# Query, value, embedding and output products issued between attention blocks, and xT moved by 1,088 bytes

## The chip, the cores and the metric

The kernel runs on one core of one Trainium2 chip. The metric is the time of one execution on the device in microseconds (us), as a median of several runs. Engines: TensorE (PE in the profile, PEld for its weight loads), VectorE (DVE), ScalarE (ACT), GpSimd (POOL), SyncE (SP, which here issues the DMAs).

## The reference

A decoder trunk of two layers on 1,024 tokens of width 1,024, in float32. Layer 0 mixes tokens with a causal convolution module, layer 1 with sliding-window attention (window 128, blocks of 128 tokens, 16 query heads on 4 key-value heads of width 64, a learned sink per head). After each mixer come a layer norm, a squared-ReLU MLP, a layer norm and a gated embedding. The attention:

```python
def swa_sink_attention(x, w_q, sinks, w_o, kk, vv, cos, sin):
    q = partial_rope((x @ w_q).reshape(B, T, N_HEADS, HEAD_DIM), cos, sin)
    q = q.reshape(B, nb, BLOCK, N_KV_HEADS, Q_PER_KV, HEAD_DIM)
    scores = jnp.einsum("bnqkgd,bnskd->bnkgqs", q, kk) * (1.0 / math.sqrt(HEAD_DIM))
    scores = jnp.where(mask, scores, -jnp.inf)
    lse = jnp.logaddexp(jax.nn.logsumexp(scores, axis=-1, keepdims=True), sink)
    probs = jnp.exp(scores - lse)
    out = jnp.einsum("bnkgqs,bnskd->bnqkgd", probs, vv)   # vv: previous and own block
    return out.reshape(B, T, N_HEADS * HEAD_DIM) @ w_o
...
x = layer_norm(DEEPNORM_ALPHA * x + y, mix_ln_g[i], mix_ln_b[i])
x = layer_norm(DEEPNORM_ALPHA * x + sq_relu_mlp(x, mlp_w_up[i], mlp_w_down[i]), ...)
x = x + (p[i] @ ple_w_proj[i]) * jax.nn.sigmoid(x @ ple_w_gate[i])
```

## The kernel before, in words

Precision. Each float32 operand is split into a high and a low part (`split`, `prep`: a rounded copy on ACT, the difference on VectorE), and a product is three matmuls per tile of 128 rows (`mm3`: high by high, high by low, low by high). `xTh` and `xTl` hold the transposed activations, 8 x 1,024 columns each; `wh` and `wl` are five slots each for prepared weights, taken in order from one stream (`ws.add`, `ws.get`, `ws.done`).

Order. The kernel's text is not the order of issue. Every operation, including the allocation of each buffer, is recorded, and a planner in the kernel (`schedule`) goes through them with costs per operation, picking for each free engine the ready operation that stands earliest in the text. The result is a fixed order for each engine's queue, which the chip then follows in order. So where an operation stands in the text sets its priority: what stands later is used where nothing earlier is ready. All instructions are issued from one helper line, 454 in the profile of before, so groups are told apart by buffers.

Attention before. Key and query weights are laid out so that a weight unit gives 128 rows: two units for the rotated parts, three (`rest(0)`) for heads 0 to 7, three (`rest(1)`) for heads 8 to 15. `part_rows(u, h)` makes one product of 24 matmuls for one half h of the tokens (512); `keep_query` scales and splits it and stores it to DRAM (`qdh`, `qdl`, buffers A). Values (`vf`, buffers g) are eight products of 24 matmuls with 256 columns, one per 128 tokens. Then three PSUM banks pass from the tag `ps` to the blocks (`sc`, `pv`).

The blocks run in two passes, gp = 0 for heads 0 to 7 and gp = 1 for heads 8 to 15, each over eight blocks n of 128 tokens and two groups of four heads. For one block and group: `load_queries` (X, from DRAM, high part in the lower 64 partitions and low part in the upper), `load_keys` (E), `load_values` (v and bo), `scores` (matmuls ps<-E,X; a copy, a predicated copy, two reduces, four exponentials, a reciprocal, four scalings into z), and, one step later, `values` (four transposes ident,z; split to A; a masked copy by GpSimd; four matmuls A by v and bo; adds into t). Pass 0 stores its result to DRAM (`adh`, `adl`), since xT is still needed by the query products; pass 1 writes to rows 4 to 7 of xT directly.

Between the passes stands `rest(1)`. After both, the result of pass 0 is loaded into rows 0 to 3 of xT, the embedding product of layer 1 is made (`embed`, 16 tiles of six matmuls, stored to `proj`), the residual x is loaded (`xsp` to B and A), and `mix_out` makes the output product: first columns 0 to 511 (cc 0) for all pairs of token tiles, then columns 512 to 1,023 (cc 1), each followed by the residual add, the second by the layer norm.

Constants (`cst`, `ident`, `mhalf`) lie just below xTh and xTl in SBUF.

## Time and profile before

| | us |
|---|---|
| median of 3 runs | 2252.42 (2250.50 to 2253.15) |
| the profiled execution, its own time | 2252.04 |
| its span, first to last instruction | 2250.3 |
| TensorE busy | 2190.7 (97%) |
| VectorE busy | 1651.6 (73%) |
| ACT busy | 891.4 (40%) |
| GpSimd busy | 244.7 (11%) |

Busy shares are averages over stages. The span in slices shows each engine's share in tenths in 40 equal stretches of 56 us; PEclk is the clock that TensorE was granted. A wait is put down to what ended it. Matmuls are pipelined and their ends are modelled, so busy TensorE time may hold less work than it seems.

### The profile page before, as it was taken

What the parts mean: (1) busy time and instruction counts of PE and PEld (TensorE: products, weight loads), DVE (VectorE), ACT (ScalarE), POOL (GpSimd) and SP (SyncE); (2) the same over time, 40 slices, a digit from 0 to 9 for tenths busy, and PEclk for the clock granted to TensorE, in tenths of its full rate; (3) what the DMA queues carried; (4) which work ended last, traced back from release to release, by engine and by line L of the source; (5) the groups of instructions that cost most, each with busy time, mean ns of one, the idle gap of its engine ahead of it and who ended that gap; (6) DMA issues with size and microseconds to landing.
All of it is one profiled execution on the core that took longest, in us unless ns stands there. A gap on an engine that the chain in (4) does not pass through costs nothing.

```text
span 2250.3 us, 28661 instructions
## 1 busy us (share of the span) xinstructions
PE 2190.7 (97%) x10187; PEld 1804.0 (80%) x10187; DVE 1651.6 (73%) x2478; ACT 891.4 (40%) x1552; POOL 244.7 (11%) x431
## 2 busy tenths in 40 slices
PE   9999999999999999999999777999999999999999
PEld 7888878888888888888889555788888888888887
DVE  7666777977778887898454839379677779778983
ACT  5233433444443333444324727334344433333341
POOL 0000134100000000003001616032000000000040
PEclk9999999999999999999999879999999999999999
DMA  7444632244449644523565472423344486454322
GB/s 224 115 109 99 193 111 90 89 164 148 152 157 329 215 141 160 187 75 103 170 195 152 132 217 80 146 86 125 115 152 150 154 285 242 166 169 164 116 68 99
DMA packets 188704, 339.95 MB, mean 151 GB/s; under 512 B 19216, under 2 KB 84240, under 8 KB 188560
## 3 DMA queue, kind: packets, MB, share of 16 engines
q1 hardware_dynamic: 187264, 337.32, 46.4%
q8 instruction: 80, 1.31, 0.2%
q10 hardware_dynamic: 1296, 0.79, 0.1%
q14 instruction: 64, 0.52, 0.1%
HBM read 234.23 MB, written 103.81 MB: 150 GB/s over the span
## 4 chain that ended last, share of the span: by engine, by line
PE 45%; DVE 5%; DMA 2%; ACT 1%; issue 1%; SPq 0%; POOL 0%; ACTq 0%; DVEq 0%
PE ps L454 29%; PE tr L454 15%; DVE sm L454 1%; DVE A L454 1%; DVE t L454 1%; DVE xTl L454 1%; ACT z L454 1%; DVE z L454 0%; DVE B L454 0%; DVE wl L454 0%; DMA qdh<-A 0%; DMA X<-qdl 0%; DMA proj<-t 0%; ACT t L454 0%; DMA X<-qdh 0%
## 5 line engine op out<-in xcount | busy, mean ns | idle before, releaser
L454 PE MATMUL ps<-xTl,wh 128*128 128x512 f32 x744 | 295.7, 398 | 0.0
L454 PE MATMUL ps<-xTh,wl 128*128 128x512 f32 x744 | 295.0, 397 | 0.0
L454 PE MATMUL ps<-xTh,wh 128*128 128x512 f32 x744 | 294.3, 397 | 0.1
L454 DVE TENSOR_TENSOR wl<-raw,wh 128x1024 fp32r<-128x1024 f32 (+2 forms) x138 | 152.7, 1107 | 127.6 <-ACT wh L454 126.8
L454 PE MATMUL ps<-xTl,xTh 128*128 128x512 f32 x618 | 240.4, 389 | 0.0
L454 PE MATMUL ps<-xTh,xTl 128*128 128x512 f32 x618 | 240.4, 389 | 0.0
L454 PE MATMUL ps<-xTh 128*128 128x512 f32 x618 | 240.4, 389 | 0.0
L454 ACT CAST wh<-raw 128x1024 fp32r<-128x1024 f32 (+2 forms) x138 | 128.9, 935 | 278.4 <-PE ps L454 124.7
L454 PEld LDWEIGHTS ps<-xTh,wh 128*128 128x128 f32 x744 | 140.4, 189 | 32.9 <-ACT xTh L454 0.9
L454 PEld LDWEIGHTS ps<-xTh,wl 128*128 128x128 f32 x744 | 140.2, 188 | 32.4
L454 PEld LDWEIGHTS ps<-xTl,wh 128*128 128x128 f32 x744 | 140.1, 188 | 31.7 <-DVE xTl L454 0.2
L454 POOL TENSOR_SCALAR sm<-sm 128x1 f32<-128x1 f32 x40 | 14.5, 363 | 1387.1 <-DVE sm L454 1385.5
L454 PE MATMUL ps<-wl,xTh 128*128 128x512 f32 (+1 forms) x392 | 150.5, 384 | 0.0
L454 PE MATMUL ps<-wh,xTh 128*128 128x512 f32 (+1 forms) x392 | 150.0, 383 | 0.3 <-ACT xTh L454 0.3
L454 PE MATMUL ps<-wh,xTl 128*128 128x512 f32 (+1 forms) x392 | 149.8, 383 | 0.0
L454 PEld LDWEIGHTS ps<-xTh,xTl 128*128 128x128 f32 x618 | 116.1, 188 | 24.1
L454 PEld LDWEIGHTS ps<-xTh 128*128 128x128 f32 x618 | 116.0, 188 | 24.1
L454 PEld LDWEIGHTS ps<-xTl,xTh 128*128 128x128 f32 x618 | 116.0, 188 | 24.0
L454 ACT CAST xTh<-wh 128x1024 fp32r<-128x1024 f32 x74 | 77.4, 1046 | 123.1 <-PE ps L454 56.8
L454 DVE TENSOR_TENSOR wl<-g,wh 128x512 fp32r<-128x512 f32 x100 | 66.5, 687 | 74.0 <-ACT wh L454 74.0
L454 ACT CAST wh<-g 128x512 fp32r<-128x512 f32 x100 | 59.8, 620 | 152.3 <-PE ps L454 67.3
L454 DVE TENSOR_TENSOR E<-cst,g 128x1152 fp32r<-128x1152 f32 x64 | 86.1, 1353 | 45.1 <-PE ps L454 44.2
(285 smaller groups left out, 4973.4 us busy)
## 6 DMA issues: line engine op xcount, KB each, us to landing
wh<-hid SPq DMA_DIRECT2D x76, 512.0 KB, 4.2
raw<-in_w_up_dram SPq DMA_DIRECT2D x64, 512.0 KB, 3.5
wl<-in_w_down_dram SPq DMA_DIRECT2D x64, 512.0 KB, 4.6
hid<-zz SPq DMA_DIRECT2D x84, 256.0 KB, 2.8
hid<-t SPq DMA_DIRECT2D x78, 256.0 KB, 2.1
raw<-hid SPq DMA_DIRECT2D x34, 512.0 KB, 3.8
B<-scr SPq DMA_DIRECT2D x32, 256.0 KB, 4.1
t<-proj SPq DMA_DIRECT2D x32, 256.0 KB, 3.4
```

What stands on the lines that cost most here:

```text
L454: getattr(getattr(nc, o.eng), o.name)(*a, **k)
```

## The change

In the text of `attention`, work moves from before, between and after the blocks to places inside the loop over blocks:

- The query products of heads 0 to 7 are made for the first token half ahead of the blocks, and for the second half (`rest(0, n, (1,))`) after blocks 0, 1 and 2 of pass 0. Since each weight unit is now used twice, three units are loaded and prepared a second time.
- Two of the eight value products come ahead of the blocks, the other six after blocks 0, 2 and 4.
- The query products of heads 8 to 15 come after blocks 3, 4 and 5 of pass 0, the embedding product (its copies now in buffers B) and the residual loads of tiles 0 to 3 after block 7.
- The result of pass 0 is loaded into xT block by block inside pass 1.
- In pass 1 the first half of the output product (cc 0) starts: tiles 0 and 1 after block 2, tiles 2 and 3 after block 4. The remaining pairs and cc 1 follow the blocks.
- `cst` grows from 272 to 544 columns, of which the added ones are not used. Thereby xTh moves from byte 162,624 of each partition to 163,712, and xTl from 195,392 to 196,480.

```diff
+CST = 256 + NT * 32 + 2 * NH
...
-        self.cc = self.const("cst", (P, 256 + NH), F32)[:, 0 : 32 + 64 + CG]
+        self.cc = self.const("cst", (P, CST), F32)[:, 0 : 32 + 64 + CG]
...
-        ws.add(*[d["w_k"][k] for k in range(2)], *[d["w_q"][k] for k in range(5)], *[d["w_v"][k] for k in range(2)])
-        ws.add(*[d["w_q"][k] for k in range(5, 8)])
+        unit = d["w_q"]
+        ws.add(*[d["w_k"][k] for k in range(2)], *[unit[k] for k in range(5)], *[d["w_v"][k] for k in range(2)])
+        ws.add(*[unit[k] for k in range(2, 8)])
...
-        def rest(s):
-            for c in range(1, 4):
-                u = ws.get(1)[0]
-                for h in range(2):
-                    self.keep_query(self.part_rows(u, h), 1 + 3 * s + c, s * HT + c, 4, h)
-                ws.done(1)
+        def rest(s, c, halves):
+            u = ws.get(1)[0]
+            for h in halves:
+                self.keep_query(self.part_rows(u, h), 2 + 3 * s + c, s * HT + c + 1, 4, h)
+            ws.done(1)
...
+        def beside(gp, n):
+            if gp == 0:
+                if n < 3:
+                    rest(0, n, (1,))
+                if n % 2 == 0 and n < 6:
+                    value_rows(n + 2)
+                    value_rows(n + 3)
+                    if n == 4:
+                        ws.done(2)
+                if 3 <= n < 6:
+                    rest(1, n - 3, (0, 1))
+                if n == 7:
+                    self.embed(1, (0, 1), "B")
+                    self.load_residual(range(0, 4))
+                return
+            if n == 1:
+                ws.add(*[d["w_o"][0, u] for u in range(4)])
+                self.ou = ws.get(4)
+            if n in (2, 4):
+                self.out_tiles(0, PAIRS[n // 2 - 1], self.ou)
...
             for n in range(NT):
                 tk = slice(n * P, (n + 1) * P)
+                if gp:
+                    for x, v in zip((self.xTh, self.xTl), self.ad):
+                        nc.sync.dma_start(
+                            x.bitcast(F32)[:, 0:4, tk], v.rearrange("p (k t) -> p k t", k=4)[:, :, tk]
+                        )
                 keys = self.load_keys(n, gp)
...
-            if gp == 0:
-                rest(1)
+                beside(gp, n)
         self.values(*pend)
...
-        self.embed(1, (0, 1), "t")
...
-        self.mix_out(1, d["w_o"], gb, range(NT))
+        self.load_residual(range(4, 8))
+        for g in PAIRS[2:]:
+            self.out_tiles(0, g, self.ou, last=g is PAIRS[-1])
+        ws.add(*[d["w_o"][1, u] for u in range(4)])
+        us = ws.get(4)
+        for g in PAIRS:
+            self.out_tiles(1, g, us, gb, last=g is PAIRS[-1])
+
+    def out_tiles(self, cc, g, us, gb=None, last=False):
+        nc = self.nc
+        for ps, t in zip(self.tok_group(g, us, last=last), g):
+            xt = self.x[t][cc]
+            nc.vector.scalar_tensor_tensor(out=xt, in0=xt, scalar=ALPHA, in1=ps, op0=ALU.mult, op1=ALU.add)
+            if cc:
+                self.layer_norm(t, gb, self.mid[1])
```

More of the change, by code (lines that the diff above doesn't have):

```diff
@@ L1408, in attention @@
         nc, d, ws = self.nc, self.d, self.ws
-        ac = self.sb("cst", n=256 + NH)
+        ac = self.sb("cst", n=CST)
         nc.sync.dma_start(ac[:, 0:256], d["aconst"])
@@ L1426, in attention, with value_rows @@
         ws.done(4)
-        def rest(s):
-            for c in range(1, 4):
-                u = ws.get(1)[0]
-                for h in range(2):
-                    self.keep_query(self.part_rows(u, h), 1 + 3 * s + c, s * HT + c, 4, h)
-                ws.done(1)
-        rest(0)
+        def rest(s, c, halves):
[3 more added lines that the diff above has]
+            ws.done(1)
+        for c in range(3):
+            rest(0, c, (0,))
         vf = [self.sb("g") for j in range(4)]
-        us = ws.get(2)
-        for t in range(NT):
+        vu = ws.get(2)
+        def value_rows(t):
             ps = self.ps()[:, 0:256]
             self.mm3(ps, [
-                (*self.xs(kb, t * P, P), *[w[:, kb % 4 * 256 : (kb % 4 + 1) * 256] for w in us[kb // 4]])
+                (*self.xs(kb, t * P, P), *[w[:, kb % 4 * 256 : (kb % 4 + 1) * 256] for w in vu[kb // 4]])
                 for kb in range(KB)
@@ L1444, in attention @@
             nc.scalar.copy(vf[t // 2][:, t % 2 * 256 : (t % 2 + 1) * 256], ps)
-        ws.done(2)
+        for t in range(2):
+            value_rows(t)
         moves = ("ps", "sc"), ("ps", "sc"), ("ps", "pv"), ("bo", "v"), ("bo", "v")
@@ L1449, in attention @@
             nc.move(a, b)
+        def beside(gp, n):
[18 more added lines that the diff above has]
+                self.out_tiles(0, PAIRS[n // 2 - 1], self.ou)
+        self.x = [None] * NT
         pend = None
@@ L1468, in attention, with load_residual @@
             nc.move(b, a)
-        for q in range(4):
-            tk = slice(q * 256, (q + 1) * 256)
-            for x, v in zip((self.xTh, self.xTl), self.ad):
-                nc.sync.dma_start(x.bitcast(F32)[:, 0:4, tk], v.rearrange("p (k t) -> p k t", k=4)[:, :, tk])
-        self.embed(1, (0, 1), "t")
-        self.x = []
-        for t in range(NT):
-            xt = [self.sb("BA"[t // 4]) for q in range(2)]
-            for q in range(2):
-                nc.sync.dma_start(xt[q], self.xsp[t // 4][t % 4 * P : (t % 4 + 1) * P, q * HT : (q + 1) * HT])
-            self.x.append(xt)
         self.hid_tags = ("X", "E")
         gb = self.load_row("g", d["mix_g"][1:2]), self.load_row("g", d["mix_b"][1:2])
-        self.mix_out(1, d["w_o"], gb, range(NT))
+        self.load_residual(range(4, 8))
[5 more added lines that the diff above has]
+            self.out_tiles(1, g, us, gb, last=g is PAIRS[-1])
+    def load_residual(self, tiles):
+        nc = self.nc
+        for t in tiles:
+            self.x[t] = [self.sb("BA"[t // 4]) for q in range(2)]
+            for q in range(2):
+                nc.sync.dma_start(self.x[t][q], self.xsp[t // 4][t % 4 * P : (t % 4 + 1) * P, q * HT : (q + 1) * HT])
+    def out_tiles(self, cc, g, us, gb=None, last=False):
+        nc = self.nc
+        for ps, t in zip(self.tok_group(g, us, last=last), g):
[3 more added lines that the diff above has]
+                self.layer_norm(t, gb, self.mid[1])
     def scores(self, n, g, q, keys):
```

## The prediction

> **What bounds the kernel now.** I read the page first: busy times, then the span in slices.

> ```profile
> span 2250.3 us, 28661 instructions
> PE 2190.7 (97%) x10187; PEld 1804.0 (80%) x10187; DVE 1651.6 (73%) x2478; ACT 891.4 (40%) x1552; POOL 244.7 (11%) x431
> PE   9999999999999999999999777999999999999999
> DVE  7666777977778887898454839379677779778983
> PEclk9999999999999999999999879999999999999999
> ```

> TensorE bounds the kernel everywhere but in slices 23 to 25, about 1,240 to 1,400 us: the attention blocks. There alone its share falls to 7 tenths and the granted clock falls with it. VectorE reads 8, 3, 9 there: first and last slice full of blocks, the middle one without. So I cut the trace into stretches (busy time of each engine in each stretch). A product takes 24 matmuls; a "unit" below is one block of 128 tokens with one group of four heads, 32 units in two passes of 16.

> ```profile
> 1178.30:1483.40 305.10, 256.46 (x1249) 207.54 (x1248) 173.91 (x364) 148.28 (x392) 91.62 (x221) 0.90 0.50 144
> 1217.75:1275.77 58.02, 47.51 (x243) 37.63 (x242) 51.04 (x114) 43.50 (x124) 32.05 (x79) 0.92 0.59 155
> 1324.00:1339.71 15.71, 1.32 (x7) 0.76 (x5) 3.49 (x9) 2.11 (x7) 0.00 (x0) 0.61 1.10 275
> 1339.71:1391.45 51.74, 39.58 (x191) 30.75 (x192) 45.83 (x105) 38.31 (x115) 29.85 (x75) 0.85 0.48 120
> 1428.50:1483.40 54.90, 54.90 (x241) 45.06 (x240) 19.02 (x23) 7.93 (x9) 0.00 (x0) 1.00 0.26 83
> ```

> Columns: length, then busy us and count of PE, weight loads, DVE, ACT, POOL, then clock, DMA share, GB/s. The first row is the stretch that the change rewrites. Its start, 1178.30, is where the two built programs part: the same number of query and key products lies before it in both. Its end, 1483.40, is a point with the same work behind it in both: the first half of the output product (cc 0, eight tiles) and the first pair of the second half are done. Rows two and four are the first and the second pass of blocks: VectorE busy 88% and 89%, TensorE 82% and 76% at a reduced clock. So in the blocks VectorE sets the pace. Row three is a plain stall: the wait table names it.

> ```profile
> PE ps L454 <- DMA X<-qdl: 14.4, 1, 14.4
> ```

> The second pass waits 14.4 us for its queries, which go through DRAM.

> **The change, part by part.** It moves TensorE work that needs nothing from the blocks into the blocks: three query products of the second token half, six of the eight value products, six query products of heads 8 to 15, the embedding product (96 matmuls), and half of the output product. No product is dropped or added. So the sum is the length of the same stretch, made from TensorE's and VectorE's work. Prices at full clock come from the chain of waits, which lists runs of matmuls back to back:

> ```profile
> 1195.30 2.83 PE tr L454 x24
> 1310.10 5.61 PE ps L454 x24
> ```

> A value product (24 matmuls of 256 columns) takes 2.83 us, 0.118 each; a query product 5.61. The output product takes 54.90 us for 240 matmuls by the last stretch row above, 0.2287 each. TensorE's whole work in the stretch: 9 query products 50.5; 8 value products 22.6; the embedding 96 x 0.2287 = 22.0; the output 54.9. The blocks, whose counts stand in these groups:

> ```profile
> L454 PE MATMUL ps<-E,X 128*128 128x256 f32 x224 | 48.1, 340 | 10.1 <-DVE z L454 7.1 <-PE ps L454 1.2 <-ACT z L454 0.8
> L454 PE MATMUL ps<-ident,z 128*128 128x128 f32 x128 | 32.2, 316 | 8.8 <-POOL z L454 8.4 <-DMA E<-kdl 0.3
> L454 PE MATMUL tr<-A,bo 128*128 128x512 f32 x76 | 30.6, 482 | 11.8 <-DVE t L454 10.9 <-DVE A L454 0.5 <-ACT A L454 0.3
> L454 PE MATMUL tr<-A,v 128*128 128x512 f32 x44 | 18.0, 474 | 2.9 <-DVE t L454 2.5 <-POOL A L454 0.3
> ```

> 224 x 0.118 = 26.4; 128 transposes and 32 narrow scores, priced at most like the 256-column ones, 18.9; 120 x 0.2287 = 27.4: 72.7, or 2.27 per unit. These rows also show why the blocks look fuller than they are: 48.1 us busy for work of 26.4, half of it pipeline ends and half clock. Total 222.7 us. Against 305.1 the most that better placing can bring is 82.4 us.

> VectorE's price of a unit comes from its groups (same window, 1,190 to 1,460):

> ```profile
> L454 DVE TENSOR_REDUCE sm<-z 128x4 f32<-128x516 f32 x64 | 43.5, 682 | 1.9 <-ACT z L454 0.8
> L454 DVE TENSOR_TENSOR t<-t,tr 64x256 f32<-64x256 f32 x64 | 27.1, 424 | 10.6 <-ACT t L454 8.9
> L454 DVE COPY_PREDICATED z<-cst,ps 128x256 f32<-128x256 int32 x56 | 23.8, 440 | 3.2 <-ACT z L454 2.2
> L454 DVE TENSOR_TENSOR A<-ps,A 128x512 fp32r<-128x512 f32 x32 | 21.8, 685 | 3.4 <-ACT A L454 3.0
> L454 DVE TENSOR_TENSOR wl<-raw,wh 128x1024 fp32r<-128x1024 f32 x10 | 12.7, 1266 | 30.3 <-ACT wh L454 30.2
> L454 DVE TENSOR_TENSOR xTl<-t,xTh 128x256 fp32r<-128x256 f32 x16 | 7.6, 473 | 2.9 <-ACT xTh L454 2.8
> L454 DVE RECIPROCAL sm<-sm 128x4 f32<-128x4 f32 x32 | 5.5, 170 | 0.2
> ...
> L454 DVE TENSOR_TENSOR bo<-g,bo 128x128 fp32r<-128x128 f32 x10 | 2.8, 282 | 2.8 <-ACT bo L454 2.8
> L454 DVE TENSOR_TENSOR bo<-t,bo 128x128 fp32r<-128x128 f32 x9 | 2.5, 278 | 0.4 <-ACT bo L454 0.4
> L454 DVE TENSOR_TENSOR v<-t,v 128x128 fp32r<-128x128 f32 x5 | 1.9, 388 | 0.0
> L454 DVE TENSOR_TENSOR v<-g,v 128x128 fp32r<-128x128 f32 x6 | 1.8, 296 | 0.8 <-ACT v L454 0.8
> L454 DVE TENSOR_TENSOR t<-g 128x128 f32<-128x128 f32 x4 | 1.1, 285 | 2.3 <-ACT g L454 2.2
> ```

> Two reduces, two adds, two predicated copies, two splits and a reciprocal make 4.42 us; the value splits, the last five rows, 10.1 us over 32 units, add 0.32: 4.75. TensorE needs 2.27 for the same unit: each unit leaves 2.5 us of TensorE free, which the moved work can fill.

> How the moved work is spread is read from the order of the built program, in three parts.

> Part A runs from the start of the stretch to the first scores of the second block of pass two. It holds 18 units less their tails (36.3 us of TensorE) and almost all of the moved work (nine query and eight value products, the embedding, five output matmuls: 96.2): 132.5 us of TensorE. VectorE has there 17 units whole (80.8), nine query splits at about 0.69 (6.2; the 685 ns of the fourth row) and ten weight splits at 1.27 (12.7), 99.7. TensorE bounds it. In-order queues don't run at 100%, so I bound the share from two rows in which moved-in work stands beside blocks already, the start of pass one and the end of pass two:

> ```profile
> 1220.00:1230.00 10.00, 10.00 (x63) 8.80 (x62) 7.22 (x16) 5.85 (x18) 3.18 (x10) 1.00 0.79 219
> 1391.45:1416.20 24.75, 20.73 (x98) 16.11 (x97) 20.09 (x47) 19.36 (x55) 15.49 (x34) 0.93 0.29 87
> ```

> 100% and 84%. I take 94%, nearer the first, since there as in part A query products were the filler: 141.0 us; bounds 132.5 and 157.7.

> Part B, the next six blocks (12 units): VectorE 12 x 4.75 plus two weight splits of 1.27, 59.5; TensorE 27.3 plus 117 output matmuls, 54.0. VectorE bounds it again, at the 88.6% of row four: 67.2; bounds 59.5 and 74.

> Part C, the end: the last units' TensorE work 9.1 and 118 output matmuls 27.0, which need earlier tokens or the heads of pass one: 36.1. The last unit's chain lies beside them, so 37.2 at 97%.

> Two hand-overs through DRAM are now shorter of cover. The first: in the trace of before the last needed query store was issued at 1190.36, and SyncE issued seven high parts ahead of the first low part:

> ```profile
> 1190.36 0.32 SPq L454 DMA_DIRECT2D qdh<-A  x1
> 1192.39 4.81 SPq L454 DMA_DIRECT2D X<-qdh  x7
> 1197.25 1.27 SPq L454 DMA_DIRECT2D X<-qdl  x2
> X<-qdl SPq DMA_DIRECT2D x13, 128.0 KB, 4.2
> ```

> Store to landing is 1197.25 + 0.6 + 4.2 - 1190.4, nearly 12 us. The built order keeps the seven ahead and puts two value products and 20 matmuls of a query product in between, 10.3 us: a wait of 2 us. The second, into pass two, before (the chain of waits):

> ```profile
> 1315.79 0.61 ACT A L454
> 1339.71 4.78 PE ps L454 x20
> ```

> From the copy of the last product to the first scores it took 23.9 us, with the DMA share at 1.10 in row three of the stretches. Now 41 embedding matmuls (9.4) and four units (9.1) of TensorE work stand in between, while the smaller reloads of xT (128 tokens each) still stand ahead of those loads in SyncE's queue: 0 to 7 us, I take 3. Behind these waits on TensorE's own queue stand the fillers, so a late transfer delays them too.

> What else moves: the residual loads of tiles 0 to 3 now start inside pass two, the weight preparations (splits on ACT and VectorE) beside blocks; The change also adds work: three weight units of the queries are loaded and prepared twice, 3 x 1.27 = 3.8 us of VectorE (among the ten splits of part A), at most as much of ACT (a copy of the same tile), and 1.5 MB of loads. With them VectorE has 177.7 us, ACT about 152, or 61% of the new length. I cost these at nothing: part A leaves VectorE 33 us, and B's two splits are in the sum. If TensorE did not cover A's ten splits, they would cost 12.7 us.

> Sum: 141.0 + 67.2 + 37.2 + 2 + 3 = 250.4 us against 305.1: 54.7 us less. The profiled execution took 2252.04 us, 0.4 below the median 2252.42; from the median that is 2197.7, say **2198**. With all terms at their ends this case runs from 2178 to 2222.

> The granted clock is in the stretch rows: 0.92 and 0.85 in the passes, 0.61 in the stall, 1.00 where TensorE has no holes. The passes have no single wait like the 14.4 us, only many short ones (4.0 to 11.8 us in all per group above), and still lose clock; so part B, with TensorE at 80%, may lose some too, which the 88.6% of row four contains. [...]

> **Rivals.** *The address.* The padding moves xTh from byte 162,624 of a partition to 163,712 and xTl by the same 1,088; everything else that feeds TensorE keeps its address. The old starts lie 64 bytes off a multiple of 128; all weights lie on one. Two stretches of 40 us at full clock, both with xT moving: the first with weights from xT itself, the second with weights from wh and wl:

> ```profile
> 750.00:790.00 40.00, 40.00 (x178) 33.11 (x177) 33.20 (x43) 13.66 (x17) 0.00 (x0) 1.00 0.55 184
> 1550.00:1590.00 40.00, 40.00 (x173) 32.25 (x172) 37.20 (x59) 15.49 (x26) 0.00 (x0) 1.00 0.24 79
> ```

> 178 against 173: 2.9%, some 6.5 ns per matmul. If the unequal offset is the cause, the shift removes it for 2,808 matmuls of the second sort in the whole program: 18.3 us, time 2179. Against it: distance in memory or neighbours could be the cause as well, and then the shift does nothing; no row varies the offset alone. [...]

> *A poor fit of the fixed order.* TensorE's queue is in order; where VectorE is later than planned, TensorE waits at a block's matmul with filler ready behind it. If A and C run at the 84% of the end of pass two and B at the 76% of TensorE's share in row four: 157.7 + 70.6 + 43.0 + 9 = 280.3, gain 25, time 2228.

> *Slower: SyncE's queue.* Nine query stores now stand among the loads of blocks. If at each the queue held back loads needed next by a whole product and the issue (5.61 + 0.6), 55.9 us, and the 14.4 us stall stayed, the stretch would be 250.4 + 70.3 = 320.7: 2268. It decides once loads are issued less than one product ahead of their block. In the built order the X loads stand in runs of about seven, several blocks ahead, which speaks against it.

> **From this to the numbers.** The forecast case 52%, the address 27%, the poor fit 16%, SyncE 5%. The likeliest gives 2198. The range 2168 to 2222 holds the first two cases with their spread and part of the third. About 0.2% (4.5 us) is what a measurement of this kernel can tell from no change: faster 0.95, same 0.01, slower 0.04.

> **What would show it.** Right: one stretch of about 250 us in place of 305.1 with TensorE's share above 85%, a clock near 1.00 in part A, no wait of TensorE for X above 7 us, VectorE near 89% in the last six blocks. The address: more than 176 matmuls per 40 us in the first-token-half products of the second MLP. Wrong: TensorE idle behind X loads, or VectorE below 80% with TensorE below 85% in the same stretch.

## The result, and the profile after

The changed kernel takes 2171.74 us (median of 4 runs, 2170.19 to 2175.14) against 2251.69 us before (4 runs, 2250.50 to 2253.15): a ratio of 0.9647, 95% interval 0.9630 to 0.9663. That is 80 us less, inside the range given and 26 us below the value forecast.

The profiled execution took 2170.38 us. Its page, busy times and slices (all instructions stand on line 455 now, one lower than before):

```profile
span 2168.7 us, 28684 instructions
PE 2147.9 (99%) x10187; PEld 1788.7 (82%) x10187; DVE 1649.9 (76%) x2480; ACT 893.3 (41%) x1555; POOL 252.6 (12%) x432
PE   9999999999999999999999999999999999999999
DVE  7667686987777977889555777899677688878983
PEclk9999999999999999999999999999999999999999
```

The three sevens in TensorE's row and the dip of the clock are gone. TensorE does the same 10,187 matmuls in 2147.9 us, 42.8 less than before; the other 38.8 of the span's 81.6 us are idle time that went.

The same stretches of work as in the prediction, busy time by engine. Row one is the whole rewritten stretch, between the two points that the two programs share; rows two to four are its parts A (with the first hand-over), B and C; row five stands at the place of the row 1550 to 1590 of before.

```profile
1168.63:1407.96 239.33, 230.20 (x1249) 192.28 (x1248) 174.49 (x365) 148.77 (x394) 99.37 (x222) 0.99 0.71 198
1168.63:1310.00 141.37, 136.80 (x781) 117.34 (x779) 92.07 (x188) 85.94 (x220) 52.86 (x118) 0.99 0.78 215
1310.00:1369.89 59.89, 56.12 (x294) 44.92 (x292) 53.39 (x123) 42.66 (x125) 31.28 (x75) 0.97 0.76 207
1369.89:1407.96 38.07, 37.28 (x178) 30.03 (x177) 29.03 (x56) 20.18 (x50) 15.23 (x30) 1.00 0.36 118
1474.03:1514.03 40.00, 40.00 (x178) 33.15 (x177) 36.84 (x58) 15.93 (x27) 0.00 (x0) 1.00 0.25 80
```

The stretch took 305.10 us and now takes 239.33, 65.8 less. TensorE's idle time in it, length less busy, fell from 48.6 to 9.1 us. But 15.8 us were gained outside it: 9.7 ahead (its start moved from 1178.30 to 1168.63) and 6.2 behind (2250.3 - 1483.40 = 766.9 before, 2168.7 - 1407.96 = 760.7 now), where nothing is placed anew. Row five points to the cause: 178 matmuls in 40 us where before had 173.

The wait table of TensorE in the stretch (us in total, times, longest):

```profile
PE ps L455 <- DVE z L455: 3.3, 1, 3.3
PE ps L455 <- DMA X<-qdl: 2.8, 1, 2.8
PE ps L455 <- POOL z L455: 1.6, 1, 1.6
PE tr L455 <- ACT xTh L455: 0.8, 1, 0.8
```

The 14.4 us wait for the second pass's queries is gone; the wait for X that is left, 2.8 us, is the first hand-over.

The longest wait left, 3.3 us for z, begins with a weight load. These are waits of ACT and of VectorE at the same place, about 1,310 to 1,314 us:

```profile
ACT wh L455 <- DMA raw<-in_w_o_dram: 3.8, 1, 3.8
DVE v L455 <- ACT v L455: 3.6, 1, 3.6
```

ACT's queue holds the rounding of an output weight (`wh`) ahead of the value splits (`v`). The weight's load, issued at 1307.49, landed 5.25 us later, so ACT stood at it, VectorE waited for the splits, and TensorE waited for the scores behind them.

### The profile page after: what moved, and what is told of

Its sections match the earlier page's. It is cut to its first block, busy times and chain, and to the rows that moved or that the text cites. A ratio compares the mean times of both kernels' runs of the same rounds, so it can differ in the third digit from the quotient of the medians.

```text
span 2168.7 us, 28684 instructions
## 1 busy us (share of the span) xinstructions
PE 2147.9 (99%) x10187; PEld 1788.7 (82%) x10187; DVE 1649.9 (76%) x2480; ACT 893.3 (41%) x1555; POOL 252.6 (12%) x432
## 4 chain that ended last, share of the span: by engine, by line
PE 44%; DVE 3%; DMA 3%; SPq 1%; ACT 1%; issue 1%; POOL 0%; DVEq 0%; ACTq 0%; POOLq 0%
PE ps L455 31%; PE tr L455 13%; SPq L455 1%; DVE xTl L455 1%; DVE A L455 1%; DVE wl L455 0%; DMA B<-xsp 0%; ACT z L455 0%; DVE B L455 0%; DVE sm L455 0%; DMA qdh<-A 0%; DVE t L455 0%; DMA X<-qdh 0%; DMA adl<-t 0%; DMA A<-xsp 0%
## 5 line engine op out<-in xcount | busy, mean ns | idle before, releaser
L455 PE MATMUL ps<-xTl,xTh 128*128 128x512 f32 x636 | 247.4, 389 | 0.0
L455 PE MATMUL ps<-xTh,xTl 128*128 128x512 f32 x636 | 247.4, 389 | 0.0
L455 PE MATMUL ps<-xTh 128*128 128x512 f32 x636 | 247.4, 389 | 0.0
L455 PE MATMUL ps<-wh,xTh 128*128 128x512 f32 (+1 forms) x408 | 156.8, 384 | 0.3 <-ACT xTh L455 0.3
L455 PE MATMUL ps<-wl,xTh 128*128 128x512 f32 (+1 forms) x408 | 156.6, 384 | 0.0
L455 PE MATMUL ps<-wh,xTl 128*128 128x512 f32 (+1 forms) x408 | 156.5, 384 | 0.0
L455 DVE TENSOR_TENSOR E<-cst,g 128x1152 fp32r<-128x1152 f32 x64 | 86.1, 1352 | 43.5 <-PE ps L455 42.6
```

The source lines that it names most:

```text
L455: getattr(getattr(nc, o.eng), o.name)(*a, **k)
```

## The experiments

Each is compared with runs of the kernel before on the same chip (medians 2252.3 to 2252.8; beside the changed kernel it was 2251.7, so times of two versions from two chips compare to about 1 us).

### Which part is the address, which the placement

Four kernels are the kernel before with another width of `cst`, so that only xTh, xTl and the two small constants under them move; a fifth is the changed kernel with the old width.

```
a1: cst 272 -> 544 columns (xT +1,088 bytes, as in the change)
a2: cst 272 -> 288 columns (xT +64 bytes)
a3: cst 272 -> 560 columns (xT +1,152 bytes)
a7: cst 272 -> 320 columns (xT +192 bytes)
b1, the changed kernel:
-CST = 256 + NT * 32 + 2 * NH
+CST = 256 + NH
```

> The kernel before with one edit: cst 544 columns instead of 272, so that xTh and xTl stand where the changed kernel has them (1,088 bytes higher, now on a multiple of 128). Order of instructions as before. Theory 1 (TensorE is slow where the starts of its two operands differ modulo 128, weights being on a multiple of 128): about 18 us less than before (2,808 matmuls x 6.5 ns), 2233.5. Theory 2 (the shift does nothing; the 15.8 us outside the rewritten stretch come from the other order): 2251.7, within 2 us. Theory 3 (distance between xT and its neighbours matters): also about 2233.5; told apart by the next two runs.

> The kernel before with cst 288 columns: xTh and xTl 64 bytes higher, on a multiple of 128 as in the changed kernel, but next to their old place. Theory 1 (offset modulo 128): as the run above, about 2233.5. Theory 3 (distance): as before, 2251.7.

> The kernel before with cst 560 columns: xTh and xTl 1,152 bytes higher, so that they stand 64 bytes off a multiple of 128 as before, but further away than in the changed kernel. Theory 1 (offset modulo 128): no change, 2251.7, and 173 matmuls per 40 us in the second MLP's first products. Theory 3 (distance): about 2233.5.

> The changed kernel with cst back at 272 columns, so that xT has its old address: the placement alone. If address and placement add, the time is that of the changed kernel plus about 18 us: 2190, 62 us below before. If the address gained nothing: 2171.7. If the two interact (TensorE's faster matmuls let it run out of filler earlier, or the slower ones are hidden beside VectorE in the blocks): 2180 to 2186.

> The kernel before with cst 320 columns: xTh and xTl 192 bytes higher, a multiple of 256, while the weights stand 128 off one. So the starts of xT and weights are equal modulo 128 and differ by 128 modulo 256. If the offset counts modulo 128: no penalty, as with a shift of 64 or 1,088 bytes, about 2233. If it counts modulo 256 with a price that grows or stays with the distance (64 one way cost 2 ns per matmul, 64 the other way 6 ns): some 4,200 matmuls at 2 to 6 ns or more dearer, 2241 to 2260.

Measured: a1 2234.58 us (ratio 0.9921, 0.9904 to 0.9938), a2 2232.39 (0.9907, 0.9891 to 0.9924), a3 2247.59 (0.9975, 0.9965 to 0.9984), a7 2253.56 (1.0006, 0.9994 to 1.0017), b1 2190.63 (0.9724, 0.9709 to 0.9738).

So the address alone brings 18.2 us and the placement alone 62.2; they add up to the 80 of the change. A step of 64 bytes does what one of 1,088 does (20.4 us in a2, 18.2 in a1), so the distance to the neighbours is not it. But my rule, equal starts modulo 128, fell too: a7 meets it and gains nothing, and a3, which breaks it as before does, gains 5.2 us. Each kernel's row at the place of that 40 us stretch, in the order a1, a2, a3, a7, b1:

```profile
1538.74:1578.74 40.00, 40.00 (x179) 33.10 (x178) 36.37 (x59) 15.97 (x28) 0.00 (x0) 1.00 0.25 79
```

```profile
1537.25:1577.25 40.00, 40.00 (x178) 33.10 (x178) 36.75 (x58) 16.02 (x27) 0.00 (x0) 1.00 0.25 79
```

```profile
1543.63:1583.63 40.00, 40.00 (x176) 32.82 (x175) 37.07 (x59) 15.39 (x26) 0.00 (x0) 1.00 0.26 79
```

```profile
1549.76:1589.76 40.00, 40.00 (x174) 32.44 (x173) 37.37 (x59) 15.48 (x26) 0.00 (x0) 1.00 0.25 79
```

```profile
1487.71:1527.71 40.00, 40.00 (x173) 32.24 (x172) 37.09 (x59) 15.50 (x26) 0.00 (x0) 1.00 0.25 80
```

Read the count of PE: 179, 178, 176, 174, 173. To see the rule I took from the traces the mean time from the start of one 512-column matmul to the next where they follow without a hole (at most 300 ns apart), sorted by the start of the moving operand minus that of the stationary one, modulo 256 bytes. The starts are those of the built programs: weights and most buffers lie at 128 modulo 256. All other 512-column matmuls, among them the products of xT with itself, have equal starts in every kernel; they are the last column.

| kernel | xT modulo 256 | xT moving, weights stationary (2,770 spacings) | weights moving, xT stationary (1,454) | equal starts |
|---|---|---|---|---|
| before | 64 | difference 192: 233.3 ns | 64: 229.3 | 227.2 |
| a3 | 192 | 64: 229.5 | 192: 233.3 | 227.3 |
| a7 | 0 | 128: 232.5 | 128: 232.8 | 227.1 |
| a1, a2, changed | 128 | 0: 227.2 to 227.4 (all pairs together) | 0 | 227.2 to 227.4 |

In these runs the price goes by the difference modulo 256: none at 0, some 2 ns at 64, 5.5 at 128, 6 at 192. Priced so, before pays 2,772 x 6.1 + 1,454 x 2.1 = 20.0 us, a3 15.2 and a7 22.8: against before 4.8 less and 2.8 more, where 5.2 less and 1.2 more were measured. At equal starts all 20.0 go; a1 and a2 gained 18.2 and 20.4. In the changed kernel half of the spacings are of pairs that differ by 256 modulo 512: 227.8 ns against 227.0 for the other half, so a difference of 256 cost under 1 ns. All this was seen in 512-column matmuls alone: the value products with their 256 columns (weights moving, xT stationary) follow one another after 118 ns at a difference of 64 in before and after 120 ns at equal starts in a1.

So in these runs the spacing depends on the start of the one operand relative to the other (227.2 to 233.3 ns): in time the two are not independent here. Which of them is held up, and by what, no run shows.

Where in the program the address counts is seen in a1's rewritten stretch:

```profile
1168.95:1472.19 303.24, 255.65 (x1249) 208.82 (x1248) 174.14 (x364) 147.94 (x392) 92.37 (x221) 0.90 0.50 145
```

It is 1.9 us shorter than before's 305.10, the rest of the program about 16. That is what the prices give: of the stretch's 1,249 matmuls only the 216 of the query products (difference 192) and the 240 of the output products (64) had unequal starts that cost, 216 x 6.1 + 240 x 2.1 ns = 1.8 us. The blocks' own 256- and 512-column matmuls, whose operands are E, X, A, v and bo, have equal starts in both kernels and had nothing to gain. So this row doesn't show what a faster matmul is worth where VectorE sets the pace.

The placement alone, b1: the stretch and its parts A, B, C.

```profile
1179.23:1421.16 241.93, 232.18 (x1249) 192.89 (x1248) 174.61 (x365) 149.19 (x394) 100.90 (x222) 0.98 0.71 196
1179.23:1322.58 143.35, 138.33 (x780) 118.14 (x779) 92.39 (x189) 86.38 (x220) 54.22 (x118) 0.98 0.77 213
1322.58:1382.76 60.18, 56.16 (x294) 44.85 (x292) 53.25 (x122) 42.61 (x125) 31.42 (x75) 0.97 0.80 207
1382.76:1421.16 38.40, 37.69 (x178) 29.90 (x177) 28.97 (x56) 20.20 (x50) 15.26 (x30) 1.00 0.37 117
```

The stretch is 63.2 us shorter than before and starts where before's did. These rows are what the forecast's sum is to be held against.

### Undoing the placement, one product at a time

b2 takes the output products out of pass two, b3 puts the six query products of heads 8 to 15 behind the last block of pass one, b5 puts the embedding behind the first half of the output product.

```
b2:  -            if n in (2, 4):
     -                self.out_tiles(0, PAIRS[n // 2 - 1], self.ou)
     ...
     -        for g in PAIRS[2:]:
     +        for g in PAIRS:
b3:  -                if 3 <= n < 6:
     -                    rest(1, n - 3, (0, 1))
                      if n == 7:
     +                    for c in range(3):
     +                        rest(1, c, (0, 1))
b5:  -                    self.embed(1, (0, 1), "B")
     ...
     +        self.embed(1, (0, 1), "t")
              ws.add(*[d["w_o"][1, u] for u in range(4)])
```

> The changed kernel, but no output product inside pass two: all pairs of the first half follow the blocks. It takes the 117 output matmuls (26.6 us) out of the last blocks and leaves the rest. If VectorE bounds those blocks, as the forecast has it, they get shorter only by the output's own VectorE work there (residual adds and statistics, 4.7 us) and the products stand behind: plus 22 us, 2194. If TensorE bounded them (it is at 94% there), the products only change their place: 2172 to 2176.

> The changed kernel with the six query products of heads 8 to 15 (33.7 us of TensorE) after the last block of pass one, not beside blocks 3 to 5. In the built order blocks 3 to 6 hold 225 matmuls, not 351. By the forecast's sums these blocks fall to VectorE's pace (eight units at 4.75 us, some 40 us against 35 of TensorE work): plus 5, 2177. If the wait for the second pass's queries comes back too, since their stores are now late: up to 14.4 more, 2191. If TensorE's sum alone counts: 2172.

> The changed kernel, but the embedding product is placed after the first half of the output product, not beside the last block of pass one. By the forecast's sums: the last block of pass one and the first of pass two fall back on VectorE's pace (9.8 us shorter with 21.9 us of embedding taken out) and the embedding stands behind: plus 12, 2184. If the embedding also covered the hand-over of the queries into pass two, a wait of TensorE for X of 5 to 9 us appears there: 2189 to 2193. If pure placement by TensorE's sum: 2172.

Measured: b2 2181.07 us (ratio 0.9685, 0.9670 to 0.9699), b3 2186.94 (0.9720, 0.9699 to 0.9741; runs 2181 to 2194), b5 2187.09 (0.9710, 0.9695 to 0.9724). Each is slower than the changed kernel, by 9, 15 and 15 us. The traced run of b3 is its fastest, 10.7 us slower than the traced run of the changed kernel. Their stretches, and for b2 part B, in the order b2, b3, b5:

```profile
1171.27:1418.70 247.43, 232.22 (x1250) 192.92 (x1248) 174.85 (x364) 148.73 (x394) 98.49 (x223) 0.99 0.69 192
1313.38:1369.40 56.02, 45.97 (x244) 36.13 (x242) 48.75 (x114) 41.80 (x123) 31.21 (x77) 0.97 0.83 215
```

```profile
1167.68:1417.88 250.20, 236.22 (x1249) 194.49 (x1248) 175.21 (x366) 149.47 (x394) 97.53 (x221) 0.97 0.67 191
```

```profile
1170.98:1425.51 254.53, 237.84 (x1250) 198.52 (x1248) 174.85 (x366) 149.56 (x394) 95.36 (x221) 0.96 0.63 178
1294.83:1365.35 70.52, 61.33 (x322) 49.85 (x321) 64.35 (x149) 51.27 (x153) 39.53 (x99) 0.95 0.58 149
```

b2 came 13 us below the 2194 expected, and was a weaker edit than the expectation said: in the built order only 50 of the 117 output matmuls left part B (x244 against x294), since the planner takes later text as filler where nothing earlier is ready. With that it fits VectorE as B's bound: 50 matmuls less (11.4 us of TensorE) shorten B by 3.9 us only, and C grows by 11.2, from 38.07 to 1418.70 - 1369.40 = 49.30. Part of the output's own VectorE work left B with them (busy 48.75 us against 53.39), so the row doesn't isolate the one from the other.

b5 came 3 us above the 2184 of VectorE's pace (row two: blocks of pass two without the embedding), and no wait for X appeared at the start of pass two, so the rival in its expectation fell. b3 missed: 15 us, not 5, and its longest wait for X is 1.3 us, so the 14.4 us stall did not return either. The loss of the traced run is split in two, which the rows show: TensorE's idle time is 250.20 - 236.22 = 14.0 us against 9.1 (plus 4.9), and the same matmuls take 236.22 us against 230.20 (plus 6.0) at a clock of 0.97 against 0.99. In b5 it is plus 7.6 and plus 7.6. By the traces' clock records TensorE ran at half clock for 6.8 us of the stretch in the changed kernel, 13.7 in b3 and 20.5 in b5; half of the difference, 3.4 and 6.8 us, is the most that the clock can have cost (at half clock 512-column matmuls follow one another after 427 ns in the traces of before and of the changed kernel, against 227 at full clock). The rest of the longer busy time can be modelled pipeline ends. Three windows of 10 us of b3, the 3.41 us ahead of the clock's drop, the time at half clock, and the longest wait in its stretch 1252 to 1320:

```profile
1250.00:1260.00 10.00, 8.80 (x51) 6.87 (x49) 9.53 (x23) 8.53 (x25) 6.04 (x15) 1.00 0.37 108
1260.00:1270.00 10.00, 7.37 (x20) 4.97 (x21) 9.08 (x19) 6.59 (x19) 6.64 (x14) 0.59 0.67 202
1270.00:1280.00 10.00, 10.00 (x41) 8.14 (x41) 4.63 (x11) 3.20 (x9) 2.21 (x5) 0.89 0.50 168
1258.46:1261.87 3.41, 1.21 (x6) 0.63 (x5) 3.29 (x10) 3.21 (x9) 2.25 (x6) 1.00 0.48 145
1261.87:1272.11 10.24, 8.61 (x23) 5.97 (x22) 9.23 (x20) 6.24 (x18) 5.63 (x12) 0.50 0.71 222
```

```profile
PE ps L455 <- POOL z L455: 1.5, 1, 1.5
```

No hole here is longer than 1.5 us, and the clock falls to half for 10.24 us: two holes, of 1.5 and 0.7 us, had left TensorE busy for 1.21 of the 3.41 us ahead, 35%. So the block without filler cost twice here: the waits, 2.2 us, and 10.24 us at a clock of 0.50 behind them.

### The added work, and the first hand-over

b7 loads and prepares the three repeated weight units once more, unused. b8 holds them in their slots from the first half to the second, so that nothing is done twice. b4 puts a third value product ahead of the blocks. c1 is b8 and b4 together.

```
b7:  -        ws.add(*[unit[k] for k in range(2, 8)])
     +        ws.add(*[unit[k] for k in (2, 2, 3, 3, 4, 4, 5, 6, 7)])
     ...
                          rest(0, n, (1,))
     +                    ws.get(1)
     +                    ws.done(1)
b8:  -        ws.add(*[unit[k] for k in range(2, 8)])
     +        ws.add(*[unit[k] for k in range(5, 8)])
     ...
     -            u = ws.get(1)[0]
     +            u = qu[c] if s == 0 else ws.get(1)[0]
     ...
     -            ws.done(1)
     +            if halves != (0,):
     +                ws.done(1)
     ...
     +        qu = ws.get(3)
b4:  -        for t in range(2):
     +        for t in range(3):
                  value_rows(t)
     ...
     -                    value_rows(n + 2)
     +                    if n:
     +                        value_rows(n + 2)
```

> The changed kernel with the three repeated weight units of the queries loaded and prepared once more (three loads of 0.5 MB, three casts on ACT, three splits on VectorE), unused. It doubles the work that the change adds. Forecast: part A has VectorE and ACT to spare, so nothing: 2171 to 2173. If TensorE's fillers do not cover them: plus 3.8 us, 2175.5. If the weight slots or SyncE's queue hold the next unit back: more, with a wait of TensorE for wh or wl.

> The changed kernel, but the three weight units of the queries of heads 0 to 7 are held in their slots from the first token half to the second, not loaded and prepared twice. It takes away what the change adds: three loads, three casts on ACT, three splits on VectorE. Forecast's step (they cost nothing): 2171.7, within 2 us. By the run with three more of them (plus 6.7): up to 6.7 less, 2165 to 2169. If the held slots keep the units of heads 8 to 15 back: slower, with TensorE waiting for wh or wl in blocks 3 to 5 of pass one.

> The changed kernel with three value products ahead of the blocks, not two, and the third no longer beside block 0. It fills the first hand-over (a wait of TensorE for X of 2.8 us) with 2.83 us of TensorE work that has no need of the blocks. If the wait is fixed in time (store to landing): 2.8 us less, 2169. If part A has no filler to lose and waits elsewhere instead: 2171.7, within 1 us.

> The changed kernel with both edits: the three units held, and three value products ahead of the blocks. If they add: the sum of the two runs before, 2163 to 2169. If they fill the same hole: as the better of the two.

Measured: b7 2178.47 us (ratio 0.9681, 0.9665 to 0.9698), b8 2174.82 (0.9653, 0.9639 to 0.9667), b4 2172.53 (0.9641, 0.9627 to 0.9656), c1 2170.61 (0.9639, 0.9625 to 0.9654). The last three cannot be told from the changed kernel's 0.9647; no version beats it by more than the runs scatter.

So taking the repeated preparations away (b8) gains nothing that shows, as forecast, though three of the five weight slots are then held, and no run tells whether that costs what the other saves. Three more of them cost 6.7 us, more than their 3.8 us of VectorE. This row is the start of b7's stretch up to the first block's scores; the same part of the changed kernel takes 1181.86 - 1168.63 = 13.23 us:

```profile
1168.90:1187.21 18.31, 13.86 (x79) 12.05 (x77) 5.18 (x8) 7.08 (x12) 0.00 (x0) 0.91 0.93 235
```

5.1 of b7's 5.9 us in the stretch (245.24 us against 239.33) stand ahead of the first scores, with 9 matmuls more there, TensorE idle for 4.5 us against 2.8, and the clock at 0.91. The edit also changed the order at that place, so what of it is the preparations' own price stays open.

b4 gained nothing, and the wait that it was to fill is still there. Its wait table names no X, but ahead of the first scores TensorE stands for 3.53 us, put down to no cause ("issue"); the changed kernel stood there for 2.76:

```profile
1182.90 1.09 PE L455 MATMUL tr<-E,X 128*128 128x128 f32 x4 [3.53 <-issue]
```

Twelve matmuls more stand ahead of it (80 against 68), but SyncE issued the first load of X at 1174.82 and not at 1172.54. Why the loads moved along, these runs don't say. In b2, b3 and b5, too, the same hole (2.7 to 3.5 us) carries no cause. The stretches of b4 and c1 are

```profile
1168.74:1409.82 241.08, 232.19 (x1250) 192.88 (x1248) 174.55 (x366) 150.02 (x394) 101.02 (x221) 0.98 0.71 197
```

```profile
1170.71:1408.38 237.67, 229.95 (x1250) 191.63 (x1248) 173.85 (x365) 148.46 (x393) 100.42 (x221) 0.99 0.69 194
```

241.08 and 237.67 against 239.33. The other long wait, for z behind the output weight, is there in both (3.8 and 3.1 us). With 9 us of idle time left in the stretch, which wait takes it is a matter of a few us that these runs don't resolve.

## Why the prediction was right and wrong

**The bound and the mechanism: right.** TensorE's work of 222.7 us was to be packed against VectorE's blocks. The stretch fell to 241.93 us at the old address (b1), TensorE's share in it is 96% (forecast: above 85%), the clock in part A 0.98 to 0.99, and b2, b3 and b5 each lose 9 to 15 us when one kind of filler is taken away.

**The sum: 8.5 us too long**, held against b1, since the forecast left the address out. Part A with the first wait: 143.0 forecast, 143.35 measured. As the 94% in it was picked between rows of 84% and 100%, so close a hit is partly luck (and that in-order queues don't run at 100% is no rule here: TensorE's was busy for 54.90 of 54.90 us in the last stretch row of before, and for 138.33 of 143.35 in b1's part A); the first wait in b1 is 3.5 us, not 2. The second hand-over: 3 forecast, no wait for X measured, and in b5, without the embedding over it, none either, so the cover was more than needed. Part C: 37.2 forecast, 38.40 measured. Part B: 67.2 forecast, 60.18 measured; this is the term that was mis-sized, by 7.0 us.

**Where B failed.** I divided a sum of VectorE's recorded durations, 59.5, by the busy share of 88.6%. The two do not belong together, because the durations overlap. In these four operations of part B of the changed kernel (start, duration),

```profile
1338.22 0.45 DVE L455 COPY_PREDICATED z<-cst,ps 128x256 f32<-128x256 int32 x1
1338.66 0.43 DVE L455 TENSOR_TENSOR xTl<-t,xTh 128x256 fp32r<-128x256 f32 x1
1339.00 0.68 DVE L455 TENSOR_REDUCE sm<-z 128x4 f32<-128x516 f32 x1
1339.60 0.68 DVE L455 TENSOR_TENSOR A<-ps,A 128x512 fp32r<-128x512 f32 x1
```

the third starts at 1339.00, before the second ends at 1339.09, and the fourth at 1339.60, before the third ends at 1339.68. Back-to-back operations overlap by some 0.08 us in the records, and the busy time of a stretch counts the overlap once. Over part B of the changed kernel the durations sum to 60.0 us in 59.89 us, 6.4 of them overlap, while the busy time is 53.39, or 89%. In row four of before (12 units of the second pass, not the whole of it) they sum to 50.8 in 51.74, 4.7 of them overlap. In the measure in which the units were priced, VectorE stood at 98% there, not at 89%: 59.5 / 0.98 is 60.7 us, within 1 us of what was measured. That does not make VectorE free of holes: in row four 5.9 us are gaps. The check that I named, VectorE near 89% in the last blocks, came true and proved nothing, as the same reading was in both. The content of the term was also not quite what I counted: 11 units, not 12, and 4.7 us of residual adds and statistics of the output product that I had left out; the two nearly cancel. And the weight preparations beside the blocks were put at nothing beyond their splits; the wait behind the output weight on ACT's queue took TensorE 3.3 us at the start of B (3.5 in b1).

```profile
L455 DVE TENSOR_REDUCE sm<-z 128x4 f32<-128x516 f32 x22 | 14.7, 679 | 0.2
...
L455 DVE BATCH_NORM_STATS2 sm<-B 128x6 f32<-128x512 f32 x3 | 2.0, 681 | 0.0
...
L455 DVE SCALAR_TENSOR_TENSOR B<-B,ps 128x512 f32<-128x512 f32 x2 | 1.4, 676 | 0.0
L455 DVE SCALAR_TENSOR_TENSOR B<-B,tr 128x512 f32<-128x512 f32 x2 | 1.3, 667 | 0.0
```

**The address: the likeliest case was wrong, the rival right.** The forecast counted the shift at nothing; the rival's 18.3 us against 18.2 in a1, and 18.9 between b1 and the changed kernel. Its rule (modulo 128) was wrong, and its sum right partly by luck: it missed the products with weights moving (3 us), and its 6.5 ns for 2,808 matmuls were 6.1 for 2,772, or 16.9 us. The row of 178 against 173 had priced it correctly before any run. What held me back was that no row varied the offset alone, and that was a reason for one sentence of doubt, not for a chance of 27%.

**The rivals that fell.** Poor fit: TensorE stands idle for 9.1 us, not for the 57.6 (280.3 less 222.7) of this case. SyncE's queue: the only wait for X is 2.8 us. Repeated preparations of the query weights: no gain without them (b8), with the reserve made there.

## What to carry to other kernels

Where a vector engine sets the pace of a loop, put matrix work without dependence beside it in the text, so that a planner has it ready there. Here this took TensorE's idle time in the stretch from 48.6 to 9.8 us (b1), and its busy time for the same matmuls from 256.46 to 232.18, with the clock at 0.98 in place of 0.90: the short holes had cost the waits, and clock too (in b3 holes of 1.5 and 0.7 us, and 10.24 us at 0.50 behind them). If work is priced by the sum of recorded durations, hold it against a sum of durations over the length of a stretch, not against a busy share, which counts overlap once. Look what stands in an in-order queue ahead of the work that others wait for: here a late weight load on ACT's queue became TensorE's longest wait, 3.3 us. If the same kind of matmul shows two spacings at full clock, compare the start addresses of its two operands modulo 256 bytes: here a shift of 64 bytes was worth 20 us of 2252.
